# A conditioned hybrid layer on one core: where adaLN's later accumulation steps and the first q, k weight splits stand

## The chip, the cores and the metric

The kernel runs on one core of a Trainium2 chip. TensorE (PE in the profile) multiplies matrices, VectorE (DVE), ScalarE (ACT) and GpSimd (POOL) work on tiles in on-chip memory, and SyncE (SP) issues the loads and stores. Each engine takes its own instructions in the order in which they were written out for it. The metric is the device time of one execution, in microseconds (us); lower is better.

## The reference, cut to what matters

The layer takes x (1024 tokens by 1024 channels) and a conditioning vector c.

```python
mod = jnp.dot(jax.nn.silu(c), w_ada) + b_ada
shift1, scale1, gate1, shift2, scale2, gate2 = split(mod, 6)          # adaLN
h = rmsnorm(x, norm1_w) * (1.0 + scale1) + shift1
proj = h @ w_in            # q, k, v; index iq, ik, iw; retention q, k, v; three gates
s_h = einsum('bqhd,bsd->bqhs', iq, ik) * idx_scale                    # index scores
score = einsum('bqh,bqhs->bqs', iw * w_scale, relu(s_h))              # causal; top 256 of them
y_a = attention over each row's top 256 keys  @ w_attn_proj
y_r = (silu(gr) * groupnorm(retention(qr, kr, vr))) @ w_ret_proj      # 4 heads, chunks of 128
x = x + gate1 * ((sigmoid(ga) * y_a + sigmoid(gb) * y_r) @ w_out)
h2 = rmsnorm(x, norm2_w) * (1.0 + scale2) + shift2
x = x + gate2 * ffn(h2);  out = rmsnorm(x, final_norm_w)
```

Only shift1 and scale1 are needed before the projections. gate1, gate2, shift2 and scale2 are needed much later: these are "adaLN's later steps".

## The kernel before, in words

**Arithmetic.** Operands of the large products are kept as a high and a low part. A weight tile arrives by a load into a raw tile (`raw_tile`, three buffers), ScalarE copies the high part (`split_weight`, L77), GpSimd subtracts for the low part (L80). The pairs live in a ring of 11 buffers. `mm_tok` makes three matmuls per slice k of the contraction: high by high (L126), high by low (L128), low by high (L129).

**Order.** The program is written out in Python, and a scheduler orders each engine's instructions by what is ready and by a priority that follows the order of writing. `turns_after(a, b)` ties `a` behind `b` on one engine, without a wait between engines. The top-k passes are written with a priority worse by `LATE`, so they fill gaps; adaLN's steps in the V stage are written with one worse by a tenth of it (`mod_step`).

**The stage of V, about 106 to 187 us.** The weights for V are eight slots; the first three of the eight slots of the next projection, q and k of the retention's first head pair (`first_qk`), are loaded and split here too, as 8 + 3 = 11 fill the ring. V is made in eight tiles of 128 tokens. The index scores run between V's matmuls. `all_scores` is a generator over query blocks 2 to 7 (`score_units`). A block turns its index queries on TensorE (L588) and copies them to `qst`, half on ScalarE (L592) and half on VectorE (L593). Then, for each of 8 heads and each chunk of keys, it makes one unit: two matmuls into an `lg` buffer (L600, L601; three buffers), a ReLU on ScalarE into `rl` (L604; three buffers), and on VectorE a sum into the score (L606 for head 0, else L608). There are 80 units. `behind_units` ties V's slices behind units, 11 units to 8 slices, from the middle of V's tile 1 on; the last units fall into the first q, k tile.

**adaLN's later steps.** `mod_work` is a generator with 32 accumulation steps, for gate1, gate2, shift2 and scale2 (indices 2, 5, 3, 4) and the eight slices k of c. A step is one VectorE instruction over 128x1024 (L701 for k = 0, else L703), `acc = mw * silu(c)[k] + acc`. It first issues the next step's load (L691, 512 KB into one of two `mw` buffers). After the eighth step a ninth call turns the sums into a gate (`mod_gate`: two products on TensorE, L749, and two additions on VectorE, L750) or into columns (`mod_cols`: transposes, L730, and reductions, L733). So the four results take 4 x 9 = 36 calls. A step is tied behind the last score sum or retention state that was written before it (`summed[-1]`); there is none yet when the steps behind V's tile 0 are written. The loads of mw are tied behind the last load of V's weights.

Before, two calls stand behind each of V's eight tiles: 16 calls, that is, gate1's nine and seven steps of gate2. Two calls stand behind each of the nine rounds of the retention's first head pair (18), and the last two are made after it.

**The retention of the first head pair, about 187 to 327 us.** First q and k in eight tiles: ScalarE scales (L852), GpSimd rotates (L861 to L866), TensorE turns (L869, L870), ScalarE and VectorE split k (L873, L874). Then V of the retention and eight chunks (`inner`, L886 to L891; `chunk`, L895 to L925), whose states `rst` VectorE adds up (L912, L914). The second head pair follows the same way. Meanwhile VectorE runs the passes of the top-k search over the scores (`select_all`, L639 to L659), one pass depending on the one before; passes 6 to 9 are tied behind chunks of the first head pair, passes 15 to 18 behind chunks of the second.

Of the kernel before, what the change touches and what calls it, by code (L numbers as in the profile page):

```python
# [43 lines left out]
def tile_hybrid_layer(ctx: ExitStack, tc: tile.TileContext, x, c, w_ada, b_ada, norm1_w, w_in,  # L44
# [20 lines left out]
    def f32(ap):  # L65
        return ap.bitcast(F32)
# [23 lines left out]
    last_load, last_split, last_low = [None], [None], [None]  # L90
# [4 lines left out]
    def rows_slot(pieces, kt, n=H, scale=None, low_behind=None, raw=None, load_behind=None, behind=None,  # L95
                  low_eng=None):

        raw = raw_tile() if raw is None else raw
        o = 0
        for w, c0, width in pieces:  # L100
            last_load[0] = nc.sync.dma_start(out=raw[:, o:o + width], in_=w[kt * P:(kt + 1) * P, c0:c0 + width])
            if load_behind is not None:
                turns_after(last_load[0], load_behind)
            o += width
        if scale is not None:
            nc.gpsimd.tensor_mul(raw[:, :n], raw[:, :n], scale)
        return split_weight(raw, n, behind=behind, low_behind=low_behind, low_eng=low_eng)
# [11 lines left out]
    def mm_tok(ps, lhs, slots, n=H, ks=None):  # L119

        last = len(slots) - 1
        head = None
        for i in ks or range(len(slots)):
            whi, wlo = slots[i]
            ahi, alo = lhs(i)
            ins = nc.tensor.matmul(ps, lhsT=ahi, rhs=whi[:, :n], start=(i == 0), stop=False)  # L126
            head = head or ins
            nc.tensor.matmul(ps, lhsT=ahi, rhs=wlo[:, :n], start=False, stop=False)  # L128
            nc.tensor.matmul(ps, lhsT=alo, rhs=whi[:, :n], start=False, stop=(i == last))  # L129
        return head  # L130

    def turns_after(ins, other):

        tc.add_manual_dep(ins.ins, other.ins.name, NOSYNC, reason="order")
# [75 lines left out]
    def ps_mm():  # L210
        return psx.tile([P, H], F32, name="mm", tag="mm", bufs=3)
# [7 lines left out]
    def big_tile(i, shape, dt, name):  # L219
        return big.tile(shape, dt, name=name, tag=f"B{i}")  # L220
# [395 lines left out]
    summed, loaded, relus = [], [], []  # L616
# [137 lines left out]
    def mod_step():  # L754
        tc.cur_priority += LATE // 10
        next(mgen, None)
        tc.cur_priority -= LATE // 10
# [8 lines left out]
    def qk_slot(hp, k):  # L766
        return rows_slot([(w_in, C_QR + 256 * hp, 256), (w_in, C_KR + 256 * hp, 256)], k,
                         behind=relus[4 * k - 33] if hp == 0 and k > 5 else None)

    first_qk = [qk_slot(0, k) for k in range(3)]  # L770
    def behind_units(mm, t, k):
        n = 11 * (KT * t + k) // 8 - 16
        if n >= 0:
            turns_after(mm, units[min(n, len(units) - 1)])

    for t in range(NT):
        ps = ps_mm()
        for k in range(KT):
            n = 11 * (KT * t + k) // 8 - 16
            while len(units) <= n and next(sgen, LATE) is not LATE:  # L780
                pass
            mm = mm_tok(ps, hT.lhs(t), slots, ks=(k,))
            behind_units(mm, t, k)
        for _ in range(2):
            mod_step()
        st = projp.tile([P, H], F32, name="vst", bufs=2)
        nc.scalar.activation(st, ps, AF.Copy)
        nc.sync.dma_start(out=v_d[:, t], in_=st)
    for _ in sgen:
        pass  # L790
    st_i.close()
    st_p.close()
    st_w.close()
# [5 lines left out]
    def ret_scale_col(kind, h):  # L799
        return rscale[:, kind * N_RET + h:kind * N_RET + h + 1]  # L800
# [9 lines left out]
    def add_up(out, terms):  # L810

        acc = ins = None
        for name, k, sign in terms:
            for part in [out] if name is None else [f32(x[:, k, :]) for x in side[name]]:
                if acc is None:
                    acc, s0 = part, sign
                    continue
                if s0 > 0:
                    step = nc.vector.tensor_tensor(out, acc, part, op=ALU.add if sign > 0 else ALU.subtract)
                else:  # L820
                    step = nc.vector.tensor_tensor(out, part, acc, op=ALU.subtract)
                ins = ins or step
                acc, s0 = out, 1
        return ins

    def alloc_side(pl, name):
        x = pl.tile([P, 2, 4, H], R, name=name, tag=name)
        side[name] = x[:, 0], x[:, 1]

    def split_sum(to, k, src):  # L830
        hi, lo = (x[:, k, :] for x in side[to])
        nc.scalar.activation(hi, src, AF.Copy)
        return nc.vector.tensor_sub(lo, src, f32(hi))

    for hp in range(2):
        slots = first_qk + [qk_slot(hp, k) for k in range(len(first_qk), KT)]
        first_qk = []
# [3 lines left out]
        for t in range(NT):  # L841
# [9 lines left out]
            for i in range(4):  # L851
                ins = nc.scalar.activation(qk[:, i], ps[:, i * P:(i + 1) * P].rearrange("p (a b) -> p a b", a=2),  # L852
                                     AF.Copy, scale=ret_scale_col(i // 2, 2 * hp + i % 2))
# [27 lines left out]
        def inner(t):  # L881
            it = ps_tr()
            for e in range(2):
                qT = qkT[t // 2][:, t % 2, e, :]
                kT = qkT[t // 2][:, t % 2, 2 + e, :]
                nc.tensor.matmul(it[:, e * P:(e + 1) * P], lhsT=kT, rhs=qT, start=True, stop=True)  # L886
            masked = retp.tile([P, 2 * P], F32, name="masked", bufs=2)
            nc.vector.tensor_mul(masked, it[:, :2 * P], rmask[:, 2 * hp:2 * hp + 2, :].rearrange("p e n -> p (e n)"))
            inns[t] = retp.tile([P, 2, 2 * P], R, name="inn", tag="qk", bufs=2)
            nc.scalar.activation(inns[t][:, 0], masked, AF.Copy)  # L890
            nc.vector.tensor_sub(inns[t][:, 1], masked, f32(inns[t][:, 0]))  # L891
# [36 lines left out]
        for t in range(NT + 1):  # L928
            if t < NT:
                ps = ps_mm()  # L930
                mm_tok(ps, hT.lhs(t), slots)
                if hp == 0:
                    both = big_tile(6 + t % 2, [P, 2, H], R, "vs")
                    vs[t] = [both[:, 0], both[:, 1]]
                else:
                    vs[t] = [ring.tile([P, H], R, name=n, tag=n, bufs=RING) for n in ("whi", "wlo")]
                nc.scalar.activation(vs[t][0], ps, AF.Copy)
                nc.vector.tensor_sub(vs[t][1], ps, f32(vs[t][0]))
                inner(t)
            if t:  # L940
                for e in range(2):
                    r[e] = chunk(t - 1, e, r[e])

            if t and t % 2 == 0:
                turns_after(passes[(5, 14)[hp] + t // 2], chunked[0])
            if hp == 0:
                if t:
                    summed.append(chunked[0])
                for _ in range(2):
                    next(mgen, None)  # L950
            elif t == 2:
                sums = [big_tile(6 + i, [P, 2, H], F32, "sums") for i in range(2)]
                sums = [x[:, i, :] for x in sums for i in range(2)]
                alloc_side(sp1, "S1")
            elif 3 <= t < 7:
                k = t - 3
                turns_after(add_up(sums[k], [("h12", k, 1), ("h22", k, 1)]), chunked[0])
                split_sum("S1", k, sums[k])
                add_up(sums[k], [(None, k, 1), ("h11", k, -1)])
# [701 lines left out]
    for hf in range(2):  # L1661
# [16 lines left out]
        for n, t in enumerate(order):  # L1678
# [23 lines left out]
            for g in range(2):  # L1702
# [5 lines left out]
                for i in range(4):  # L1708
                    k = 4 * g + i
                    h_to, h_of = hraw[th][:, g, i, o:o + P], tp[:, i * P:(i + 1) * P]  # L1710
                    sc, sh = modr[:, KT + k:KT + k + 1], modr[:, k:k + 1]
                    if k < (6 if n < 6 else 4):
                        ins = nc.scalar.activation(h_to, h_of, AF.Identity, scale=sc, bias=sh)
# [396 lines left out]
```

## Time and profile before

| what | value |
| --- | --- |
| median of 3 runs | 1681.17 us (1680.22 to 1681.71) |
| the profiled execution | 1679.94 us, its span 1678.2 us |
| busy in the span: TensorE / VectorE / ScalarE / GpSimd | 1653.3 / 1222.3 / 784.8 / 856.6 us |
| mean granted TensorE clock | 0.999 |
| first and last start of V's copies on ScalarE (L787) | 116.7 and 186.7 us |
| first and last start of the score sums (L608) | 120.8 and 203.0 us |
| first and last start of adaLN's steps (L701, L703) | 112.3 and 324.9 us |

In a timeline row stand the start, the length, the engine, the line of the kernel, what is written from what, the shapes, how often, and in brackets the idle time of the engine just before and what ended it. A windows row gives a stretch and each engine's busy time in it. In the list of waits stand the total, the count and the longest, in us.

### The profile page before, as it was taken

Reading aid. Unit: us, or ns where it says so; the run is one execution under the profiler, and the core shown is the slowest. Engines: PE = TensorE matmul, PEld = TensorE weight load, DVE = VectorE, ACT = ScalarE, POOL = GpSimd, SP = SyncE. Lnnn points to the kernel's source line nnn. Section 1 sums busy time; section 2 is a strip of 40 time slices with the busy share of each in tenths; the row PEclk is TensorE's granted clock in tenths of the full one; section 3 lists DMA queues with packets and bytes.
Section 4 is the critical chain, followed back from the end, with each engine's and each line's share of the span. In section 5 each row is a group of like instructions: output and inputs, shape, how many; then the busy total and the mean of one; then the engine's idle time right before and its main releaser. Section 6 shows DMA issues by size and latency. Waiting matters only on the chain.

```text
span 1678.2 us, 24672 instructions
## 1 busy us (share of the span) xinstructions
PE 1653.3 (99%) x8311; PEld 1383.1 (82%) x8311; DVE 1222.3 (73%) x2001; ACT 784.8 (47%) x1592; POOL 856.6 (51%) x874
## 2 busy tenths in 40 slices
PE   7999999999999999999999999999999999999998
PEld 6987788888888887888888888888888888888887
DVE  7539897988995879784775858966555566687574
ACT  4636535545552454420784347534333333445444
POOL 5660394874452885220455910245455555657573
PEclk9999999999999999999999999999999999999999
DMA  9554415412442565962956600245444443686652
GB/s 305 190 166 151 132 52 160 148 33 82 138 131 82 160 193 181 309 176 99 213 116 232 244 26 1 77 147 184 145 145 168 146 151 139 207 307 223 197 158 100
DMA packets 178653, 260.70 MB, mean 155 GB/s; under 512 B 13712, under 2 KB 109408, under 8 KB 176224
## 3 DMA queue, kind: packets, MB, share of 16 engines
q1 hardware_dynamic: 178272, 258.85, 49.3%
q8 instruction: 65, 1.06, 0.3%
q14 instruction: 60, 0.49, 0.1%
q10 hardware_dynamic: 256, 0.30, 0.1%
HBM read 192.51 MB, written 66.58 MB: 154 GB/s over the span
## 4 chain that ended last, share of the span: by engine, by line
PE 85%; DVE 8%; issue 2%; DMA 2%; ACT 1%; POOL 1%; SPq 0%; POOLq 0%; DVEq 0%; ACTq 0%
PE ya L1067 5%; PE ya L1065 5%; PE ya L1069 5%; PE yb L1065 3%; PE yb L1069 3%; PE yb L1067 3%; PE mm L126 3%; PE mm L128 3%; PE mm L129 3%; DVE eq L639 3%; PE ya L1973 3%; PE ya L1974 3%; PE ya L1975 3%; PE mm L1069 2%; PE mm L1065 2%
## 5 line engine op out<-in xcount | busy, mean ns | idle before, releaser
L80 POOL TENSOR_TENSOR wlo<-wraw,whi 128x512 fp32r<-128x512 f32 (+1 forms) x93 | 128.3, 1392 | 156.7 <-ACT whi L77 138.4
L639 DVE TENSOR_SCALAR_CACHE_REDUCE eq<-score,cand 128x384 uint8<-128x384 f32 (+2 forms) x192 | 181.0, 943 | 3.8
L980 POOL TENSOR_TENSOR flo<-tmp,fhi 128x512 fp32r<-128x512 f32 x79 | 107.9, 1366 | 140.4 <-ACT fhi L979 100.8
L128 PE MATMUL mm<-wlo,hT_hi 128*128 128x512 f32 (+1 forms) x408 | 152.6, 375 | 0.0
L129 PE MATMUL mm<-whi,hT_lo 128*128 128x512 f32 (+1 forms) x408 | 152.0, 373 | 0.0
L126 PE MATMUL mm<-whi,hT_hi 128*128 128x512 f32 (+1 forms) x408 | 151.5, 375 | 0.0
L1067 PE MATMUL ya<-hc,fhi 128*128 128x512 f32 x344 | 133.9, 389 | 0.6 <-DVE hc L1605 0.6
L1065 PE MATMUL ya<-hc,fhi 128*128 128x512 f32 x344 | 133.6, 389 | 0.3 <-DVE c L1048 0.3
L1069 PE MATMUL ya<-hc,flo 128*128 128x512 f32 x344 | 132.9, 389 | 0.0
L1949 ACT ACTIVATE dslot<-draw 128x512 fp32r<-128x512 f32 x143 | 83.9, 627 | 91.2 <-DMA draw<-act_d 27.3
L1950 DVE TENSOR_TENSOR dslot<-draw,dslot 128x512 fp32r<-128x512 f32 x81 | 91.0, 1156 | 46.0 <-ACT dslot L1949 45.9
L980 POOL TENSOR_TENSOR flo<-raws,fhi 128x512 fp32r<-128x512 f32 x60 | 86.8, 1452 | 73.2 <-ACT fhi L979 38.2
L1950 POOL TENSOR_TENSOR dslot<-draw,dslot 128x512 fp32r<-128x512 f32 x62 | 94.2, 1535 | 50.5 <-ACT dslot L1949 49.4
L979 ACT ACTIVATE fhi<-tmp 128x512 fp32r<-128x512 f32 x82 | 51.5, 629 | 111.5 <-PE ya L1067 58.0
L1065 PE MATMUL yb<-hc,fhi 128*128 128x512 f32 x256 | 99.6, 389 | 0.0
L1067 PE MATMUL yb<-hc,fhi 128*128 128x512 f32 x256 | 99.6, 389 | 0.0
L1069 PE MATMUL yb<-hc,flo 128*128 128x512 f32 x256 | 99.4, 389 | 0.0
L1033 DVE TENSOR_TENSOR tmp<-raws 128x512 f32<-128x512 f32 x40 | 30.6, 768 | 87.0 <-POOL flo L980 87.0
L77 ACT ACTIVATE whi<-wraw 128x512 fp32r<-128x512 f32 (+1 forms) x94 | 55.5, 609 | 75.3 <-DMA wraw<-in_w_in_dram 25.7
L129 PEld LDWEIGHTS mm<-whi,hT_lo 128*128 128x128 f32 x408 | 76.7, 188 | 11.7
L128 PEld LDWEIGHTS mm<-wlo,hT_hi 128*128 128x128 f32 x408 | 76.8, 188 | 10.7 <-issue 0.2
L126 PEld LDWEIGHTS mm<-whi,hT_hi 128*128 128x128 f32 x408 | 76.5, 188 | 10.9 <-PE lg L749 0.2
(495 smaller groups left out, 4950.0 us busy)
## 6 DMA issues: line engine op xcount, KB each, us to landing
draw<-act_d SPq DMA_DIRECT2D x70, 256.0 KB
mw<-in_w_ada_dram SPq DMA_DIRECT2D x32, 512.0 KB
act_d<-c SPq DMA_DIRECT2D x58, 256.0 KB
raw<-in_w_in_dram SPq DMA_DIRECT2D x26, 512.0 KB
raws<-in_w_ffn_gate_dram SPq DMA_DIRECT2D x24, 512.0 KB
raws<-in_w_ffn_up_dram SPq DMA_DIRECT2D x24, 512.0 KB
dw<-in_w_ffn_down_dram SPq DMA_DIRECT2D x22, 512.0 KB
dw_d<-dw SPq DMA_DIRECT2D x10, 1024.0 KB
```

Source lines behind the costliest of these rows:

```text
L77: last_split[0] = ins = nc.scalar.activation(hi[:, :n], raw[:, :n], AF.Copy)
L80: last_low[0] = low = (low_eng or nc.gpsimd).tensor_sub(lo[:, :n], raw[:, :n], f32(hi[:, :n]))
L126: ins = nc.tensor.matmul(ps, lhsT=ahi, rhs=whi[:, :n], start=(i == 0), stop=False)
L128: nc.tensor.matmul(ps, lhsT=ahi, rhs=wlo[:, :n], start=False, stop=False)
L129: nc.tensor.matmul(ps, lhsT=alo, rhs=whi[:, :n], start=False, stop=(i == last))
L639: ins = [nc.vector.tensor_scalar(eq[:, :sc.shape[1]], sc, thr[j], None, op0=op, op1=ALU.add, accum_out=cnt[:, j:j + 1]) for j, sc in enume ...
L980: return ins, (eng or nc.gpsimd).tensor_sub(lo, src, f32(hi))
L1065: mm = nc.tensor.matmul(ps, lhsT=whi[:, k, :], rhs=hhi[:, k, :], start=own and k == 0, stop=False, skip_group_check=True)
L1067: nc.tensor.matmul(ps, lhsT=whi[:, k, :], rhs=hlo[:, k, :], start=False, stop=False, skip_group_check=True)
L1069: nc.tensor.matmul(ps, lhsT=wlo[:, k, :], rhs=hhi[:, k, :], start=False, stop=k == 3, skip_group_check=True)
L1949: nc.scalar.activation(slot[:, 0], raw, AF.Copy)
L1950: ins = lo_eng.tensor_sub(slot[:, 1], raw, f32(slot[:, 0]))
```

## The change

The number of calls of `mod_step` behind V's tiles 0 to 7 becomes 0, 2, 2, 2, 2, 2, 1, 1 (12 in place of 16), and the first four rounds of the retention's first head pair make three calls each in place of two. So behind V's tiles now stand gate1's nine calls and the first three steps of gate2; the gate1 product moves from behind tile 4 to behind tile 5. The rounds of the retention now begin with steps 3 to 5 of gate2, then its steps 6 and 7 and the gate product, then three steps of shift2, then three more; from the fifth round on all is as it was. And the ScalarE instructions that split the first three q, k slots are tied behind the second, third and fourth ReLU (`relus[1 + k]`).

```diff
-    first_qk = [qk_slot(0, k) for k in range(3)]
+    first_qk, first_split = [], []
+    for k in range(3):
+        first_qk.append(qk_slot(0, k))
+        first_split.append(last_split[0])
+
     def behind_units(mm, t, k):
...
-        for _ in range(2):
+        for _ in range((0, 2, 2, 2, 2, 2, 1, 1)[t]):
             mod_step()
         st = projp.tile([P, H], F32, name="vst", bufs=2)
         nc.scalar.activation(st, ps, AF.Copy)
         nc.sync.dma_start(out=v_d[:, t], in_=st)
     for _ in sgen:
         pass
+    for k, ins in enumerate(first_split):
+        turns_after(ins, relus[1 + k])
...
             if hp == 0:
                 if t:
                     summed.append(chunked[0])
-                for _ in range(2):
+                for _ in range(3 if t < 4 else 2):
                     next(mgen, None)
```

## The prediction

> **What bounds the kernel now.** I read the page's busy times first, then the windows view over the stages that the edit touches, then the timelines of TensorE, ScalarE, VectorE and GpSimd in the stage of V, and at the end the chain.
>
> ```profile
> span 1678.2 us, 24672 instructions
> ...
> PE 1653.3 (99%) x8311; PEld 1383.1 (82%) x8311; DVE 1222.3 (73%) x2001; ACT 784.8 (47%) x1592; POOL 856.6 (51%) x874
> ```
>
> TensorE is busy for 1653.3 of 1678.2 us, so the time is TensorE's work plus the 24.9 us in which it stands still. Nothing in this change adds or removes a matmul. It can only move standing time. The windows (start:end and length, then busy time of PE, PEld, DVE, ACT, POOL with counts, granted clock, DMA share, GB/s) show where that is:
>
> ```profile
> 106.00:187.00 81.00, 78.02 (x367) 62.52 (x366) 68.80 (x104) 49.72 (x99) 16.65 (x16) 1.00 0.56 176
> 121.00:151.00 30.00, 29.20 (x140) 23.11 (x139) 28.95 (x46) 19.49 (x42) 0.58 (x1) 1.00 0.45 134
> 205.00:254.60 49.60, 49.60 (x234) 40.12 (x233) 48.06 (x95) 19.99 (x53) 47.55 (x65) 1.00 0.22 64
> 254.60:271.40 16.80, 16.80 (x94) 14.52 (x93) 9.45 (x19) 10.68 (x31) 7.41 (x16) 1.00 0.46 133
> 271.40:295.00 23.60, 23.60 (x130) 20.44 (x129) 22.25 (x46) 12.03 (x35) 10.66 (x27) 1.00 0.53 169
> 295.00:372.00 77.00, 76.89 (x384) 64.16 (x382) 72.90 (x139) 34.95 (x97) 64.60 (x94) 1.00 0.34 98
> ```
>
> The first row is the V stage with the index scores in it: TensorE idles 81.00 - 78.02 = 2.98 us there. From 205 to 295 us (retention of the first head pair) it idles nothing, and from 295 to 372 us 0.11. The granted clock is 1.00 everywhere, so the clock has no part in this. VectorE has next to no room in some of those rows: busy 28.95 of 30 us from 121 to 151, idle 49.60 - 48.06 = 1.54 us in 205 to 254.6, 7.35 in 254.6 to 271.4, 1.35 in 271.4 to 295.
>
> The places of the 2.98 us, in TensorE's timeline (start, length, and in brackets the idle time just before):
>
> ```profile
> 114.94 0.39 PE L129 MATMUL mm<-whi,hT_lo 128*128 128x512 f32 x1
> 115.83 0.45 PE L600 MATMUL lg<-khi,qst 128*128 128x384 f32 x1 [0.51 <-DVE qst L593]
> ...
> 116.76 0.40 PE L129 MATMUL mm<-whi,hT_lo 128*128 128x512 f32 x1
> 117.42 0.44 PE L600 MATMUL lg<-khi,qst 128*128 128x384 f32 x1 [0.27 <-DVE qst L593]
> ...
> 136.59 0.33 PE L600 MATMUL lg<-khi,qst 128*128 128x384 f32 x1
> 136.76 0.34 PE L601 MATMUL lg<-klo,qst 128*128 128x384 f32 x1
> 137.34 0.39 PE L600 MATMUL lg<-khi,qst 128*128 128x256 f32 x1 [0.24 <-ACT rl L604]
> ...
> 138.14 0.39 PE L129 MATMUL mm<-whi,hT_lo 128*128 128x512 f32 x1
> 138.74 0.45 PE L600 MATMUL lg<-khi,qst 128*128 128x384 f32 x1 [0.20 <-ACT rl L604]
> ...
> 141.78 0.45 PE L600 MATMUL lg<-khi,qst 128*128 128x384 f32 x1 [0.35 <-ACT rl L604]
> ...
> 181.58 0.39 PE L128 MATMUL mm<-wlo,hT_hi 128*128 128x512 f32 x1
> 181.80 0.39 PE L129 MATMUL mm<-whi,hT_lo 128*128 128x512 f32 x1
> 183.59 0.50 PE L600 MATMUL lg<-khi,qst 128*128 128x512 f32 x1 [1.40 <-ACT rl L604]
> ```
>
> Matmul ends are modelled, so I take starts. Two 128x512 matmuls start 0.22 us apart (181.58, 181.80) where nothing holds them, two 128x384 ones 0.17 (136.59, 136.76). By that, place A (114.94 to 115.83 and 116.76 to 117.42) loses 0.67 + 0.44 = 1.11 us, waiting for the transposed queries qst of VectorE. Place B (three score products from 137.34 to 141.78) loses 0.41 + 0.38, and 0.35 by its bracket: 1.14 us, waiting for a ReLU. Place C (183.59) loses 1.79 - 0.22 = 1.57 us, again for a ReLU. Sum 3.82 us: more than the 2.98 of the records, and the most that this stage can give back.
>
> **The change part by part.** First, two accumulation steps behind V's tile 0 go away. What they and the q, k splits do there:
>
> ```profile
> 112.33 1.33 DVE L701 TENSOR_SCALAR macc<-mw,colT 128x1024 f32<-128x1024 f32 x1 [5.64 <-DMA mw<-in_w_ada_dram]
> 113.70 1.36 DVE L703 SCALAR_TENSOR_TENSOR macc<-mw,colT,macc 128x1024 f32<-128x1024 f32 x1
> 115.09 1.28 DVE L593 TENSOR_TENSOR qst<-tr,qst 64x512 fp32r<-64x512 f32 x2
> ...
> 120.77 3.40 DVE L608 SCALAR_TENSOR_TENSOR score<-rl,iws,score 128x384 f32<-128x384 f32 x4 [1.77 <-ACT rl L604]
> ...
> 178.84 2.31 DVE L703 SCALAR_TENSOR_TENSOR macc<-mw,colT,macc 128x1024 f32<-128x1024 f32 x1
> ```
>
> ```profile
> 113.07 0.59 ACT L592 ACTIVATE qst<-tr 64x512 fp32r<-64x512 f32 x1 [1.31 <-PE tr L588]
> 114.40 0.64 ACT L77 ACTIVATE whi<-wraw 128x512 fp32r<-128x512 f32 x1 [0.73 <-DMA wraw<-in_w_in_dram]
> 114.94 0.57 ACT L592 ACTIVATE qst<-tr 64x512 fp32r<-64x512 f32 x1
> ...
> 119.59 0.63 ACT L77 ACTIVATE whi<-wraw 128x512 fp32r<-128x512 f32 x1 [1.32 <-DMA wraw<-in_w_in_dram]
> 120.25 1.26 ACT L604 ACTIVATE rl<-lg 128x384 f32<-128x384 f32 x3
> ...
> 176.24 0.63 ACT L77 ACTIVATE whi<-wraw 128x512 fp32r<-128x512 f32 x1
> ```
>
> VectorE runs two macc steps (1.33 and 1.36 us) from 112.33 to 115.06, and the two qst copies, whose ScalarE half began at 113.07 and took 0.59, start only at 115.09. Without the steps the first can start at 113.07 + 0.59 = 113.66, some 1.4 us sooner. The second half on ScalarE begins at 114.94, behind a q, k split of 0.64 us at 114.40 that itself waited 0.73 us for its load; with the split ordered behind the second ReLU, it can begin at about 113.7. So the first score product no longer waits: place A goes, -1.11 us. I take all of it; the bounds are 0 (if something else is late, such as the load of the 0.73 us) and 1.11.
>
> Second, the order of the splits. At 119.59 the third split starts after 1.32 us of waiting for its load, and takes 0.63; behind it, in the same in-order queue, stand the ReLUs of 120.25, whose score products were long ready (TensorE issued the second at 117.42). VectorE's sums (120.77) wait for those ReLUs 1.77 us. In the change the ReLUs go first. That hands VectorE a start of up to 1.32 + 0.63 = 1.95 us, and it is VectorE, fully busy in this stretch, that sets the ReLU's rl buffers free at place B. A start of 1.95 us covers B's 1.14: -1.14 us. The bounds are 0 and 1.14. The splits themselves stay: 3 times 0.63 us on ScalarE between ReLUs. That is at most 1.89 us for the ReLUs behind them; I cost it at nothing, as three lg buffers stand between ScalarE and TensorE; if that cover is gone, it eats B's gain. What the splits feed, the next loads into the three raw buffers and their splits, is not due before 176.24, where the next split stands; so their own lateness costs nothing.
>
> Third, behind tiles 6 and 7 one step instead of two. A step mostly costs 1.28 us (least, median and most in ns, over all 28):
>
> ```profile
> L703 DVE SCALAR_TENSOR_TENSOR macc<-mw,colT,macc x28: 1276/1280/2312, 113.7 to 324.9; 128x1024 f32<-128x1024 f32 x28
> ```
>
> The longest is the one at 178.84, 2.31 us. Place C comes 2.4 us behind that step, at the end of a VectorE queue without a gap. Taking out one step there gives back the lower price, -1.28 of 1.57 us; the bounds are 0 and 1.57. The adaLN gate's product moves from behind tile 4 to behind tile 5, and the second gate from the first to the second chunk of the retention: the same work on every engine, at nothing, with 0 and 0.8 (both qst waits together, 0.51 + 0.27) as bounds.
>
> Sum of the V stage: -1.11 - 1.14 - 1.28 = -3.53 us, between 0 and -3.82.
>
> Fourth, what comes back in the retention: three steps instead of two per chunk in the first four. With the gate one chunk later, the surplus over before is two steps at the first chunk, whose order ties them only to the last score sum, so that they run from about 200 us on, and one each at the third and fourth chunk, near 271 to 295. The first two are 2 x 1.28 = 2.56 us in the row with 1.54 us idle; what is over, 1.0 us, reaches the next row with its 7.35 us of idle, so they cost TensorE nothing (GpSimd's part is a rival below). The other two are 2.56 us in a row with 1.35 us idle, and 1.21 us are carried on. Behind them VectorE has the top-k passes, one after the other, up to the second head pair's retention, where the chain shows TensorE released by it:
>
> ```profile
> 371.20 0.70 DVE wlo L938
> 371.94 0.97 PE lg L895 x6
> ```
>
> There the low half of V (371.20 + 0.70) arrives as TensorE starts, after an idle of 0.11 us. No slack, so I put the 1.21 us on the path whole. Bounds: 0, if the scheduler, which ranks the passes last, puts the retention's own instructions ahead of them; and 2.56, with no idle used. The four loads (512 KB each) go with their steps through SyncE's queue, past the stores of ret_d and the next weights. The DMA share is 0.56 in the V stage and 0.22, 0.46, 0.53 in the three rows, so there is room; I cost them at nothing, with 0 and 1.3 us (the wait for a load at 119.59) as bounds.
>
> Sum: -3.53 + 1.21 = -2.32 us. The profiled execution took 1679.94 us, its span 1678.2 and 1.74 around it; the median of the runs shown is 1681.17, 1.23 above. So 1679.94 - 2.32 = 1677.6 for an execution like the profiled one, and 1681.17 - 2.32 = 1678.9 for the median.
>
> **The rivals.** (1) The retention costs nothing and the V stage gives all: -3.82, so 1677.4. For it: not one wait of TensorE between 187 and 371 us, and passes of the lowest rank. Against: 1.35 us of idle for two steps.
>
> (2) VectorE stays the limit of the V stage. Six steps remain behind tiles 1 to 3, and from 121 to 151 VectorE has hardly any idle. Then B and C come back elsewhere, A alone is won, the 1.21 us is paid: -1.11 + 1.21 = +0.1, so 1681.3. It decides if VectorE's sums are as far behind at 137 us as before.
>
> (3) Slower: the steps collide with GpSimd. They come from a stretch where it stands still into one where it is busy 47.55 of 49.60 us. The price is in these rows:
>
> ```profile
> 120.30 1.28 POOL L80 TENSOR_TENSOR wlo<-wraw,whi 128x512 fp32r<-128x512 f32 x1 [2.66 <-ACT whi L77]
> ...
> 188.39 4.17 POOL L80 TENSOR_TENSOR wlo<-wraw,whi 128x512 fp32r<-128x512 f32 x1 [6.09 <-ACT whi L77]
> ...
> 247.42 0.45 POOL L866 TENSOR_TENSOR kv<-rra,rrb 128x128 f32<-128x128 f32 x1
> ```
>
> ```profile
> 250.19 0.27 PE L869 MATMUL tr<-ident,rq 128*128 128x128 f32 x1
> ```
>
> One low part takes 1.28 us alone and 4.17 us at 188.39, across two macc steps and two score sums: 2.89 us of blocking. If each of the two early steps does that, GpSimd's rotations of q and k end 5.78 us later. TensorE turns the last of them at 250.19, 2.32 us after it is made (247.42 + 0.45); beyond these, 3.46 us are lost. The two later steps at 2.31 us are 4.62 less 1.35 idle: 3.27. Together 6.73 - 3.53 = +3.2, so 1684.4. It turns to a loss when the blocking costs TensorE more than 3.53 us. Against it: those 2.89 us lay over four VectorE instructions, not one, so half would be the fairer price.
>
> The Trainium skill has this as a rule, in "SBUF — State Buffer", section "Who interferes with whom": a VectorE instruction with two SBUF inputs contends with a GpSimd instruction that reads SBUF, and whichever issues first holds the port for the whole instruction while the other is fully blocked. By that rule alone each early step blocks GpSimd for no more than its own length, 2 x 1.28 = 2.56 us against 2.32 of cover, a loss of 0.24 us in place of the 3.46. The trace agrees that the block exists (4.17 against 1.28).
>
> **How the numbers follow.** The forecast has 0.37, rival 1 0.25, rival 2 0.20, rival 3 0.18. One figure for what a measurement of this kernel can tell from no change: 0.2%, or 3.4 us, that is below 1677.8 or above 1684.5. Rival 1 lies just past it, so four fifths of it (0.20) and the fast edge of the forecast (0.07) give faster 0.27. Half of rival 3 gives slower 0.09. The rest, 0.64, is the same. The range goes from 1676.4 (rival 1 with 1 us for starts that no bracket shows, and for an order that the scheduler redraws) to 1684.4 (rival 3). Cases of both signs have much of the chance; the forecast's own range is 1677.4 to 1680.1 (3.82 won with nothing paid, to 3.53 won with 2.56 paid).
>
> **What would show it.** After: no TensorE wait for qst at the first two score products, with VectorE's first qst right behind ScalarE's; the ReLUs 2 to 4 without a split that waits for a load between 1 and 2; no wait of a score product for a ReLU near 137 to 142 nor of over 0.3 us near 180; TensorE's idle in the V stage 0.3 us or so instead of 2.98, and V's last copy some 3.5 us earlier. In the retention, steps of 1.28 us near 200 us, GpSimd's last rotation relative to V's end not over 2.3 us later, and at the second head pair's first state product a wait of about 1.3 us for wlo in place of 0.11. Wrong would be: the same ReLU waits at other places (rival 2), TensorE waiting for the rotations or low parts of GpSimd near 245 to 260 us (rival 3), or a later stage in which the scheduler, which orders the rest anew, makes waits that no row of before shows.

## The result, and the profile after

The change made the kernel slower: 1696.65 us (median of 5 runs, 1695.56 to 1698.57) against 1680.55 us for the kernel before in the same comparison, ratio 1.0097 (95% interval 1.0085 to 1.0108). The forecast was 1678.9 us.

The profiled execution after, from the page's head, and then the windows over the same stages (columns as before). From line 771 on the changed file's line numbers are 4 higher, behind line 790 they are 6 higher: L901, L910, L918 and L920 are the chunks' L895, L904, L912 and L914 of before.

```profile
span 1694.9 us, 24672 instructions
...
PE 1658.3 (98%) x8311; PEld 1387.0 (82%) x8311; DVE 1228.1 (72%) x2001; ACT 786.0 (46%) x1592; POOL 860.6 (51%) x874
```

```profile
106.00:187.00 81.00, 79.71 (x380) 65.44 (x379) 69.27 (x104) 51.36 (x102) 18.15 (x17) 1.00 0.51 160
205.00:254.60 49.60, 46.66 (x224) 37.92 (x223) 47.62 (x96) 20.03 (x52) 46.16 (x64) 1.00 0.24 65
254.60:271.40 16.80, 16.80 (x85) 14.20 (x85) 7.05 (x11) 6.15 (x16) 5.34 (x11) 1.00 0.43 126
271.40:295.00 23.60, 23.60 (x121) 19.74 (x120) 16.00 (x28) 12.83 (x38) 10.67 (x25) 1.00 0.42 136
295.00:320.00 25.00, 21.92 (x106) 18.54 (x105) 22.44 (x37) 10.86 (x29) 17.02 (x24) 0.86 0.72 220
320.00:372.00 52.00, 50.74 (x249) 42.01 (x247) 49.38 (x96) 24.28 (x72) 44.50 (x69) 1.00 0.23 71
372.00:440.00 68.00, 62.44 (x323) 53.27 (x324) 57.74 (x117) 34.81 (x96) 30.41 (x66) 0.97 0.27 74
```

Span less TensorE's busy time is 36.6 us against 24.9: 11.7 us more standing. Busy time rose by 5.0 us with the same 8311 matmuls; some 4 us of it fall where the granted clock was low (last section). The standing and the busy time together are the 16.7 us by which the span grew. Where TensorE stands: in the V stage 1.29 us instead of 2.98, so more than half of that was won; 2.94 us from 205 to 254.6, where it stood not at all before; nothing from 254.6 to 295; then 3.08, 1.26 and 5.56 us. The last of these stretches was full before:

```profile
372.00:440.00 68.00, 68.00 (x351) 58.42 (x352) 59.09 (x114) 42.59 (x116) 38.35 (x76) 1.00 0.36 105
```

The first lines of the list of what TensorE waited for between 187 and 440 us (total, times, longest):

```profile
PE tr L892 <- DVE masked L894: 4.8, 2, 3.1
PE tr L875 <- POOL rq L872: 4.2, 2, 3.3
PE lg L910 <- DVE rst L920: 3.1, 1, 3.1
```

**The V stage** went largely as forecast. VectorE's first qst copy starts at 113.78, right behind ScalarE's half, no score product waits for qst, and the 1.40 us wait at 183.59 is gone. Three waits for a ReLU remain, two of them where place B was:

```profile
113.78 0.68 DVE L593 TENSOR_TENSOR qst<-tr,qst 64x512 fp32r<-64x512 f32 x1 [7.01 <-ACT qst L592]
...
126.47 0.50 PE L600 MATMUL lg<-khi,qst 128*128 128x512 f32 x1 [0.30 <-ACT rl L604]
...
137.76 0.44 PE L600 MATMUL lg<-khi,qst 128*128 128x384 f32 x1 [0.70 <-ACT rl L604]
...
141.10 0.38 PE L600 MATMUL lg<-khi,qst 128*128 128x256 f32 x1 [0.29 <-ACT rl L604]
```

The last score sum starts at 200.1 us, 2.9 us earlier than before (203.0).

**From 200 to 255 us** that lead is lost again. GpSimd's first rotation beside two steps of adaLN, then the same two instructions of GpSimd in before:

```profile
202.64 1.85 DVE L703 SCALAR_TENSOR_TENSOR macc<-mw,colT,macc 128x1024 f32<-128x1024 f32 x1
203.37 1.72 POOL L868 TENSOR_TENSOR rrb<-qk,sinr 128x256 f32<-128x256 f32 x1
...
205.87 1.42 DVE L703 SCALAR_TENSOR_TENSOR macc<-mw,colT,macc 128x1024 f32<-128x1024 f32 x1
206.16 1.45 POOL L871 TENSOR_TENSOR kv<-rra,rrb 128x128 f32<-128x128 f32 x1
```

```profile
206.25 0.73 POOL L862 TENSOR_TENSOR rrb<-qk,sinr 128x256 f32<-128x256 f32 x1
...
208.06 0.46 POOL L865 TENSOR_TENSOR kv<-rra,rrb 128x128 f32<-128x128 f32 x1
```

The same instructions take 1.72 instead of 0.73 and 1.45 instead of 0.46 us where a step of adaLN runs beside them: 1.98 us. GpSimd's last rotation starts at 246.50 against 247.42, only 0.92 us earlier, and TensorE waits 0.92 and 0.24 us for GpSimd and 1.69 us for a mask of VectorE. By chunk 0's first product (257.51, before 257.85) 0.34 us of the lead is left.

**From 263 us** comes the main loss. VectorE, then TensorE:

```profile
263.56 0.42 DVE L918 COPY rst<-lg 128x256 f32<-128x256 f32 x1 [2.94 <-PE lg L901]
263.90 1.27 DVE L703 SCALAR_TENSOR_TENSOR macc<-mw,colT,macc 128x1024 f32<-128x1024 f32 x1
265.69 1.28 DVE L703 SCALAR_TENSOR_TENSOR macc<-mw,colT,macc 128x1024 f32<-128x1024 f32 x1
...
272.17 0.69 DVE L750 TENSOR_TENSOR gateb<-gateb,lg 128x512 f32<-128x512 f32 x1 [5.21 <-PE lg L749]
...
277.40 0.48 DVE L920 SCALAR_TENSOR_TENSOR rst<-rst,rscale,lg 128x256 f32<-128x256 f32 x1 [3.68 <-PE lg L901]
```

```profile
271.12 1.88 PE L749 MATMUL lg<-macc,spare 128*128 128x512 f32 x4
272.83 0.59 PE L910 MATMUL lg<-rst,qkT 128*128 128x256 f32 x2
```

```profile
265.69 0.47 DVE L914 SCALAR_TENSOR_TENSOR rst<-rst,rscale,lg 128x256 f32<-128x256 f32 x1
```

Chunk 0's second state is copied at 263.56. The second gate's last two steps are tied behind it; the gate's product (L749), which needs them, comes at 271.12, and VectorE idles 5.21 us for it. Chunk 1's first product starts at 272.83 and its state at 277.40, 11.7 us later than before (265.69). TensorE does not idle meanwhile: it makes V's products for later chunks, which need no state. At 296.8 us the next product in its order needs one:

```profile
293.28 0.28 PE L901 MATMUL lg<-vs,kk_lo 128*128 128x256 f32 x1
...
296.40 0.40 PE L129 MATMUL mm<-whi,hT_lo 128*128 128x512 f32 x1
299.88 1.19 PE L910 MATMUL lg<-rst,qkT 128*128 128x256 f32 x2 [3.08 <-DVE rst L920]
...
302.57 0.63 PE L128 MATMUL mm<-wlo,hT_hi 128*128 128x512 f32 x1
303.00 0.63 PE L129 MATMUL mm<-whi,hT_lo 128*128 128x512 f32 x1
```

It stands 3.08 us for a state, and then the matmuls start 0.43 us apart instead of 0.23. V's products are not used up there: they go on behind the wait (302.57). VectorE's queue shows why this state comes so late:

```profile
291.89 1.80 DVE L703 SCALAR_TENSOR_TENSOR macc<-mw,colT,macc 128x1024 f32<-128x1024 f32 x1 [1.86 <-DMA mw<-in_w_ada_dram]
...
295.83 2.30 DVE L703 SCALAR_TENSOR_TENSOR macc<-mw,colT,macc 128x1024 f32<-128x1024 f32 x1
298.06 1.27 DVE L639 TENSOR_SCALAR_CACHE_REDUCE eq<-score,cand 128x1024 uint8<-128x1024 f32 x1
299.26 0.47 DVE L920 SCALAR_TENSOR_TENSOR rst<-rst,rscale,lg 128x256 f32<-128x256 f32 x1
```

TensorE's part of the state was issued by 293.28; VectorE had waited 1.86 us for a load and then had two steps of adaLN and passes ahead of it. The state before it, at 289.57, was only 6.6 us later than in the kernel before (283.02), this one is 14.0 (299.26, before 285.23). So the late chunk 1 alone does not make this wait; the bunched steps and a load have a part in it. At the start of the second head pair TensorE stands 3.31 us for a rotation and 3.11 for a mask. VectorE makes the first mask there at 381.88, before at 369.75.

### The profile page after: what moved, and what is told of

The parts are those of the page before. It is cut to its first block, busy times and chain, and to the rows that moved or that the text cites. A ratio compares the mean times of both kernels' runs of the same rounds, so it can differ in the third digit from the quotient of the medians.

```text
span 1694.9 us, 24672 instructions
## 1 busy us (share of the span) xinstructions
PE 1658.3 (98%) x8311; PEld 1387.0 (82%) x8311; DVE 1228.1 (72%) x2001; ACT 786.0 (46%) x1592; POOL 860.6 (51%) x874
## 4 chain that ended last, share of the span: by engine, by line
PE 84%; DVE 10%; issue 2%; ACT 2%; DMA 1%; POOL 1%; SPq 0%; POOLq 0%; DVEq 0%; ACTq 0%
PE ya L1073 5%; PE ya L1071 4%; PE ya L1075 4%; DVE eq L639 4%; PE yb L1071 3%; PE yb L1075 3%; PE yb L1073 3%; PE mm L128 3%; PE mm L129 3%; PE mm L126 3%; PE ya L1979 3%; PE ya L1981 2%; PE ya L1980 2%; PE mm L1075 2%; PE mm L1071 2%; PE mm L1073 2%
```

## The experiments

Three theories. T1: the second gate's product, written behind chunk 0 instead of ahead of it, holds up the chunks. T2: the surplus steps collide with GpSimd and fill VectorE. T3: the ties of the splits, or the new order that the scheduler draws because of them. Each time is a median with the ratio to the kernel before on the same chip, whose median lay between 1679.97 and 1680.61 us. Line numbers differ by a few between these kernels.

**1. The split ties alone.** Before plus

```diff
+    for k, ins in enumerate(first_split):
+        turns_after(ins, relus[1 + k])
```

> Only the ties of the three q, k splits behind ReLUs 2 to 4; all adaLN steps stand as before. Theory 1 (the second gate's last two steps and its product, moved behind chunk 0's state, hold two of the three lg buffers while chunk 1 waits) expects no loss here: 1678 to 1681 us, a gain of 0 to 2.5 us in the V stage. Theory 2 (the surplus steps collide with GpSimd and fill VectorE in the retention) expects the same. Theory 3 (the split ties make the scheduler redraw the order badly) expects most of the 16 us loss: over 1690.

1680.94 us, ratio 1.0003 (0.9994 to 1.0012): no change that can be told. T3 falls as far as the ties go, and so does the prediction's 1.14 us for the splits' order.

**2. The new counts alone,** without the ties.

> Only the new counts of adaLN's steps, without the ties of the splits. Theory 1 and theory 2 expect the whole loss: 1693 to 1699 us. Theory 3 expects 1678 to 1683.

1698.44 us, 1.0111 (1.0097 to 1.0125): the whole loss, with the same 3.1 us wait for rst, which ends at 299.8.

**3. The gate moved one round later in the kernel before,** its V stage untouched and no surplus step near 200 us:

```diff
-                for _ in range(2):
+                for _ in range((0, 4, 2, 2, 2, 2, 2, 2, 2)[t]):
```

> The kernel before with one thing moved: the first round of the retention makes no call, the second four, so that the second gate's last step and its product come behind chunk 0's state, with the V stage and the number of steps as before. Theory 1 expects a loss of 8 to 15 us against before: 1689 to 1696, with chunk 1's first product some 8 to 12 us after where it stood. Theory 2 expects none, as no step is added to the stretch where GpSimd is busy and one is even taken away: 1678 to 1682.

1694.21 us, 1.0083 (1.0069 to 1.0097). The time is as T1 expected, though chunk 1's first product comes at 268.95, 5.1 us later than before (263.89) and not 8 to 12. The surplus steps of T2 are not needed for a loss of this size.

**4. The changed kernel with the gate back ahead of chunk 0:** six calls in the first round, two in the others.

```diff
-                for _ in range(3 if t < 4 else 2):
+                for _ in range(6 if t == 0 else 2):
```

> The V stage of the change with the splits' ties, but all the steps taken from V go to the first round of the retention: six calls there, two in each later one. The second gate's product then stands ahead of chunk 0, as before. Theory 1 expects that the loss is gone: 1677 to 1682. Theory 2 expects more loss than in the change at the rotations, as five steps instead of three fall on GpSimd near 200 us: 1686 to 1698.

1682.13 us, 1.0014 (1.0005 to 1.0023): 0.13 us above T1's range. The waits between 295 and 440 us are gone but for 0.11 us. What is left is by its place T2's share: TensorE stands 3.04 us between 205 and 271.4, where it stood not at all before:

```profile
205.00:254.60 49.60, 48.16 (x223) 38.17 (x222) 47.17 (x93) 19.08 (x50) 48.42 (x64) 1.00 0.31 94
254.60:271.40 16.80, 15.20 (x85) 13.10 (x84) 10.71 (x20) 9.71 (x27) 7.55 (x16) 1.00 0.45 126
```

**5. The changed kernel without the second gate's product.**

```diff
-            gp = ps_lg()
+            gp = ps_lg() if i == 0 else None
...
-            nc.vector.tensor_add(g, g, gp)
+            nc.vector.tensor_add(g, g, gp if i == 0 else acc[:, cs])
```

> The changed kernel, but the second gate's product is left out: its two additions take the accumulated sums themselves instead of a product in an lg buffer (so gate2 is not the reference's). Steps 6 and 7 of that gate stay tied behind chunk 0's state. Theory 1 (the product stands in the retention's ring of three lg buffers between chunk 0 and chunk 1 and makes chunk 1 wait until step 7 is done): chunk 1's first state product back at about 263 to 266 us instead of 272.8, time 1677 to 1683 us, of which up to 1.9 us are the four matmuls left out. Rival 2 (the two steps themselves, tied behind chunk 0, delay VectorE's states): 1692 us or more, chunk 1 still near 272 us.

1691.70 us, 1.0068 (1.0056 to 1.0081). A miss for T1's time. Chunk 1's first state is on time (265.61), as T1 said, but most of the loss stays: TensorE still stands 2.99 us from 205 to 254.6, and in many waits of 0.2 to 1.6 us between 306 and 640 us. So a late chunk 1 is not needed for a large loss either. Experiment 13 prices the omission itself.

**6. The two late steps untied from chunk 0,** the product still written behind it.

```diff
-                if t:
+                if t > 1:
                     summed.append(chunked[0])
```

> The changed kernel, but the three calls of the retention's second round (steps 6 and 7 of the second gate and its product) are tied behind the last score sum like those of the first round, not behind chunk 0's state. The product is still written between chunk 0 and chunk 1. Theory 1 in its form 'the wait is for the two late steps': the steps run near 208 to 215 us, the product no longer waits, time 1679 to 1684 us. Theory 1 in its form 'the place of the product in the order of the lg buffers costs, whenever its steps are done': 1690 to 1697 us.

1689.17 us, 1.0057 (1.0043 to 1.0070), just below the second form's range. The steps now run at 208.67 and 212.51, the product follows chunk 0 at once (265.56), and chunk 1's state still comes at 272.26. So the product costs even when nothing is late for it.

**7 and 8. The steps behind V's last tile,** where VectorE has gaps of 2.42 us between score sums, and the retention's rounds as before.

```diff
-        for _ in range((0, 2, 2, 2, 2, 2, 1, 1)[t]):
+        for _ in range((0, 2, 2, 2, 2, 2, 1, 5)[t]):      # 8: (0, 2, 2, 2, 2, 2, 2, 4)
...
-                for _ in range(3 if t < 4 else 2):
+                for _ in range(2):
```

> Calls behind V's tiles 0, 2, 2, 2, 2, 2, 1, 5 (16 as before), two in every round of the retention, with the ties of the splits: the steps taken from tile 0 and tile 6 come back behind tile 7, where VectorE stands idle 2.4 us at a time between score sums (192 to 203 us of before), and the gate is written where it was before. Theory 1 with the V stage's gain kept (2.9 us earlier at its end in the changed kernel): last score sum near 200 us, no wait of TensorE for rotations, 1676.5 to 1679.5 us. Rival (the steps collide with GpSimd's low parts and rotations wherever they are put): GpSimd's last rotation at 247 us or later, 1680 to 1683 us.

> As the run with 1 and 5 behind the last two tiles, but 2 and 4: calls 0, 2, 2, 2, 2, 2, 2, 4. If tile 6's second step is what made the 1.57 us wait for a ReLU at 183.6 us of before, that wait comes back and the time is 1.0 to 1.6 us above that run; if not, the two agree within 0.5 us: 1677 to 1680 us. Rival (collisions anyway): 1680 to 1683 us.

1678.32 us, 0.9987 (0.9978 to 0.9996), and 1679.32 us, 0.9995 (0.9986 to 1.0004). With 1 and 5 the V stage's gain is kept: VectorE takes the steps in 187 to 205 us (15.37 us busy instead of 11.21) and TensorE stands nowhere from 187 to 254.6.

```profile
106.00:187.00 81.00, 79.67 (x380) 65.39 (x379) 69.34 (x104) 51.41 (x102) 18.17 (x17) 1.00 0.51 160
187.00:205.00 18.00, 18.00 (x81) 14.92 (x80) 15.37 (x21) 7.12 (x17) 7.20 (x6) 1.00 0.64 204
205.00:254.60 49.60, 49.60 (x238) 40.24 (x237) 46.89 (x93) 21.52 (x55) 46.39 (x64) 1.00 0.21 59
```

With two steps behind tile 6 a wait of 0.83 us for a ReLU returns at 182.59, and the median is 1.0 us higher (the intervals overlap): place C was priced about right, if a little high.

**9. The product's call alone,** one round later in the kernel before; the step ahead of it stays near 203 us.

```diff
-                for _ in range(2):
+                for _ in range((1, 3, 2, 2, 2, 2, 2, 2, 2)[t]):
```

> The kernel before with the rounds' calls as 1, 3, 2, 2, ...: the second gate's last step stays where it was (203.65 us), and its product alone is written in the second round, behind chunk 0, not in the first. V's stage and the early steps are as before. Theory 1b (the product's place between chunk 0 and chunk 1 in the ring of lg buffers costs by itself): chunk 1's first state 4 to 7 us later than the 265.7 us of before, as in the run with untied steps (272.3), time 1685 to 1692 us. Rival 2 (only the accumulation steps tied behind chunk 0 cost): 1679 to 1682 us.

1695.72 us, 1.0079 (1.0063 to 1.0095), by the medians 15.3 us, more than expected; one of the six runs took 1687.65 us. Moving the product's call is enough for the loss (TensorE's timeline below). Chunk 1's first state is at 272.68, 6.5 us behind chunk 0's last (266.17), in the kernel before 1.6; TensorE also stands 2.10 us for a mask at 253.75, before the moved call, since the scheduler draws the order anew, and 5.30 at the second head pair:

```profile
265.97 1.88 PE L749 MATMUL lg<-macc,spare 128*128 128x512 f32 x4
...
378.67 1.22 PE L886 MATMUL tr<-qkT 128*128 128x128 f32 x4 [5.30 <-DVE masked L888]
```

**10. One step moved, product left out** (experiment 3 with the omission of 5).

> The kernel before with the rounds' calls as 0, 4, 2, 2, ... (the run that took 1694.2 us), but with the second gate's product left out (its additions take the accumulated sums, so gate2 is not the reference's). What is left is one accumulation step (1.28 us) and two additions moved from before chunk 0 to behind it, without the two early surplus steps. Theory 1b: chunk 1 on time (265 to 267 us), 1678 to 1682 us, of which up to 1.9 us are the matmuls left out. Rival 2 (VectorE's steps behind chunk 0 push shift2's steps and what follows, whatever the product does): 1687 to 1694 us, with waits of TensorE for rotations and masks near 365 to 380 us.

1684.89 us, 1.0029 (1.0018 to 1.0039), between the two expectations; chunk 1's state at 264.18.

**11. The whole second gate before the retention:** calls 0, 2, 2, 2, 2, 2, 1, 7 and none in the first round.

> Calls behind V's tiles 0, 2, 2, 2, 2, 2, 1, 7 and none in the first round of the retention, two in each of the others: the whole second gate, product too, before the retention. Against the run with 5 behind the last tile: no step at 200.7 us beside GpSimd's first rotations, but the product's two lg buffers stand among the last score products. Theory 1 (a product does harm where a chain waits for lg buffers behind it): the score products near 195 to 200 us are not a chain, each waits only for its ReLU, so 1677 to 1679 us; rival: TensorE or the rotations wait there for the gate's additions, 1680 to 1684 us.

1700.12 us, 1.0115 (1.0102 to 1.0128). A clear miss. The product stands in TensorE's order ahead of score products, and its steps wait for their loads (the longest waits are 2.78 and 2.54 us). TensorE's timeline:

```profile
199.80 3.75 PE L749 MATMUL lg<-macc,spare 128*128 128x512 f32 x4 [15.27 <-DVE macc L703]
```

**12. Experiment 7 without the ties.**

> The run with 0, 2, 2, 2, 2, 2, 1, 5 calls, without the ties of the three q, k splits. If the ties carry a part of V's gain (in the two runs with the surplus steps V's stage idled 1.64 us without and 1.29 us with them), the time is 0.3 to 0.6 us above that run's 1678.3; by the prediction's price of 1.14 us for the splits' order it is 1.1 us above; if they carry nothing, the same within 0.3 us. 1678.0 to 1679.6 us.

1677.57 us, 0.9985 (0.9977 to 0.9994), the lowest median here and below its expected range; by their intervals this run and experiment 7 are faster than before, by little. TensorE idles 1.30 us in the V stage without the ties and 1.33 with them. Without them a score product waits 1.01 us for qst at 117.38, with them the ReLU waits are 1.3 us instead of 0.3: the ties exchange one wait for another.

**13. Leaving the product out of the kernel before.**

> The kernel before with the second gate's product left out where it stands (its additions take the accumulated sums, so gate2 is not the reference's). It prices the product itself for the two runs without it: four matmuls of 0.47 us are 1.9 us of TensorE, so 1678 to 1679 us if that is all; 1680 to 1683 us if the order of what follows is drawn worse without it, which would put a part of the 4.5 and 11.3 us of those two runs down to leaving the product out and not to the steps.

1683.47 us, 1.0016 (1.0006 to 1.0025), 0.5 us above its second range: 2.9 us slower with 1.9 us less work on TensorE. A redrawn order alone is worth some microseconds. Each measured against its own before, 10 is 1.6 us slower than this run (4.5 - 2.9), which is no more than a redrawn order can make; 5 is 8.4 us slower (11.3 - 2.9), with the collisions, two steps moved and later calls. What of these makes the 8.4 us was not tried.

**14 and 15. The product in another ring of buffers,** in the changed kernel.

```diff
-            gp = ps_lg()
+            gp = ps_lg() if i == 0 else ps_tr()      # 15: ps_mm()
```

> The changed kernel, but the second gate's product goes into the two tr buffers (ring of the transposes and of the inner products) instead of the three lg buffers. Everything else as changed. Theory 1a (the product blocks because chunk 1 needs the lg buffers that it holds): chunk 1's first state back to 263 to 267 us, time 1681 to 1687 us, unless the inner products of the next chunk then wait for the tr buffers (a wait of TensorE or of the masks near 270 us; 1688 to 1694 us). Theory 1c (not the ring, but the place in TensorE's and VectorE's order and the steps behind it): chunk 1's first state still near 272 to 277 us, 1692 us or more.

> The changed kernel, but the second gate's product goes into the three mm buffers (ring of V's products) instead of lg. Theory 1a: chunk 1's first state at 263 to 267 us; V's products, which run ahead while the gate waits, now wait behind it instead, so TensorE shows an idle stretch near 264 to 270 us; 1684 to 1692 us. Theory 1c: chunk 1's first state at 272 us or later, 1692 us or more.

1693.37 us, 1.0073 (1.0061 to 1.0086), and 1695.38 us, 1.0086 (1.0072 to 1.0101). Chunk 1's first state comes back, by VectorE's timeline, first with tr, then with mm:

```profile
264.46 0.47 DVE L920 SCALAR_TENSOR_TENSOR rst<-rst,rscale,lg 128x256 f32<-128x256 f32 x1
```

```profile
260.04 0.47 DVE L920 SCALAR_TENSOR_TENSOR rst<-rst,rscale,lg 128x256 f32<-128x256 f32 x1
```

So with other buffers for the product chunk 1 no longer waits: the ring of lg buffers held it in the changed kernel. But the time hardly follows, and T1a's times do not come out: 14 lies in the range given for waits near 270 us, but TensorE has none there, and 15 lies 3.4 us above its range, without the idle stretch at 264 to 270 us. The wait reappears elsewhere (chunk 3's first state at 289.05 with tr against 283.02 before; 2.98 us for adaLN's last sums at 331 with mm).

**What the set shows.** By the medians every version with the second gate's product behind chunk 0 loses 8.8 to 18.5 us: the changed kernel, 2, 3, 6, 9, 14 and 15. The versions that have it between the score sums and chunk 0 lie between -2.8 and +2.2 us: 1, 4, 7, 8 and 12. (11, which loses 19.7, has it ahead of the last score products.) Shown: moving the product's call behind chunk 0 brings the loss (9), putting it back ahead of chunk 0 takes it away (4, 7), its lg buffers hold chunk 1 (14, 15), and the early steps collide with GpSimd. Not shown: that the late chunk 1 is what costs the 16 us. With chunk 1 on time 12.8 and 14.8 us stay (14, 15), and without the product 11.3 (5). Open is therefore how the 16 us divide between that first wait, the moved steps and the order that the scheduler draws anew; no run held the order fixed.

## Why the prediction was wrong

- **The step that failed** is "the second gate from the first to the second chunk of the retention: the same work on every engine, at nothing, with 0 and 0.8 as bounds". Experiment 9 measured +15.3 us by the medians (10.6 to 16.0 by the interval of the ratio) for moving its product's call alone, with the order that the scheduler drew for it. The same work was indeed done; but four matmuls were put into a chain (chunk 0, chunk 1, ...) with three lg buffers, of which each chunk takes four in turn. The bound of 0.8 came from the qst waits, a place where no chain follows. How that becomes 15 us of time stays open, as said above. A row of before that could have warned is chunk 0's second state, for which VectorE stood 3.38 us waiting for TensorE; what is put ahead of a product there can move the next state too:

```profile
264.09 0.42 DVE L912 COPY rst<-lg 128x256 f32<-128x256 f32 x1 [3.38 <-PE lg L895]
```

- **Place A** (-1.11): right in kind, the wait for qst is gone. It needs both parts: with the new counts alone a wait of 1.0 to 1.4 us for qst stays (experiments 2 and 12).
- **Place B** (-1.14): wrong. By their brackets two ReLU waits of 0.99 us together stand there now (before three of 0.79), with a third of 0.30 ahead of them, and the ties are worth nothing. Rival 2 was right about this place.
- **Place C** (-1.28): right in the main; the wait is gone, 1.0 us lies between the medians of experiments 7 and 8, and the wait that returns in 8 is 0.83 us.
- **The V stage's sum** (-3.53): 2.9 us by the last score sum, 1.7 by TensorE's idle time there. Experiments 7 and 12, where the steps went elsewhere, are 2.1 and 2.8 us faster than before in all.
- **Two early steps at nothing for TensorE**: wrong. Rival 3's mechanism came, though not as the main loss: GpSimd lost 1.96 us (2.88 of lead, 0.92 left), TensorE stood 2.94, of it 1.16 for GpSimd. The rule quoted there from the Trainium skill, no more than the steps' own length (2.56), held for GpSimd's loss; the cover of 2.32 us did not. TensorE came 2.9 us earlier, and it also reached the rotations without the gate's product, which in before stood ahead of the last of them (238.81 us, 1.88 us long).
- **The later steps' 1.21 us at the low part of V** and the loads at nothing: not tried by themselves. In after a step waits 1.86 us for its load until 291.89, more than the 1.3 us bound, and this wait stands in VectorE's queue ahead of the state for which TensorE stands 3.08 us.
- **The clock**, which the prediction gave no part: about 4 us of the loss fall where the granted clock was 0.50 to 0.60 (last section).
- **What would make it wrong** named "a later stage in which the scheduler, which orders the rest anew, makes waits that no row of before shows". That happened, but it had no price and no place in the range.

## What to carry to other kernels

Before moving an instruction at nothing, ask whose ring of buffers it uses and which dependent chain is written next into that ring: a product of 1.9 us that stood free ahead of a recurrence cost 15 us inside it, with the order that the scheduler drew anew. TensorE's idle time does not show it at that place, since free work runs ahead; look for a state that arrives late (here 11.7 us), and at the first wait for a state look at what the other engine had in its queue ahead of it. Of the places tried here, accumulation steps did best where their own engine has idle gaps: with five behind V's last tile the kernel was 2.1 and 2.8 us faster than before. With seven and the product there it lost 19.7.

## What was not expected of the hardware

A wait of TensorE cost more than its length. The windows of the changed kernel around the 3.08 us wait:

```profile
297.00:300.00 3.00, 0.12 (x1) 0.15 (x1) 3.00 (x5) 0.90 (x2) 1.53 (x4) 0.82 0.71 192
300.00:303.00 3.00, 3.00 (x10) 2.63 (x11) 3.00 (x6) 1.80 (x7) 2.75 (x4) 0.50 0.98 321
303.00:306.00 3.00, 3.00 (x9) 2.37 (x8) 2.96 (x5) 2.02 (x5) 2.76 (x5) 0.55 0.91 282
306.00:309.00 3.00, 3.00 (x16) 2.46 (x14) 2.84 (x8) 0.73 (x2) 3.00 (x4) 1.00 0.88 286
...
375.00:378.00 3.00, 3.00 (x12) 2.51 (x12) 3.00 (x4) 0.60 (x1) 3.00 (x3) 0.60 0.37 87
```

The granted clock is 0.50 and 0.55 for 6 us after the wait, and back at 1.00 from 306. With a second drop at 375 to 378 us (0.60), behind the wait of 3.31 us, this makes an estimated 3 x (0.50 + 0.45 + 0.40) = 4.1 of the 5.0 us of added busy time, counting only windows in which TensorE was busy throughout. The length of a wait does not settle it. In experiment 6 a wait of 2.94 us left the clock at 1.00, and 2.10 us at 640 us left it at 1.00 in before but brought 0.55 and 0.60 over 4 us in experiment 12 (each time TensorE's timeline, then the window behind it):

```profile
248.82 0.33 PE L875 MATMUL tr<-ident,rq 128*128 128x128 f32 x1 [2.94 <-POOL rq L872]
```

```profile
249.00:252.00 3.00, 2.68 (x15) 2.10 (x15) 2.89 (x9) 1.01 (x2) 3.00 (x4) 1.00 0.17 41
```

```profile
639.24 0.50 PE L1073 MATMUL mm<-hT_hi,wlo 128*128 128x512 f32 x1 [2.10 <-POOL wlo L984]
```

```profile
640.00:642.00 2.00, 2.00 (x6) 1.50 (x5) 2.00 (x4) 0.92 (x2) 2.00 (x2) 0.55 0.77 231
```

The Trainium skill, in "TensorE: Matmul & The Clock Gate", section "Part 1: The HAM clock gate", says that the clock is halved after an idle window of some 3.4 us, and that the window runs freely. The halving agrees (0.50), and that equal waits differ fits a window that runs freely; but here waits of 2.10 and 3.08 us sufficed, less than the figure of the Trainium skill, and the measurement decides. The prediction priced a wait at its length.
